# A hybrid diffusion step on one core: the low parts of every second normalised feature tile move from VectorE to GpSimd

## The chip, the cores and the metric

The kernel runs on one core of a Trainium2 chip. Five engines work side by side, each on its own list of instructions: TensorE (PE, matmuls), VectorE (DVE), ScalarE (ACT), GpSimd (POOL) and SyncE (SP), which in this kernel issues nearly all transfers between DRAM and the on-chip memory. An instruction waits until those of other engines that it depends on have ended. The metric is the time of one execution in microseconds, as the device measures it, median of several runs.

## What is computed

One inference step of a two-layer backbone for 640 tokens (128 context tokens, 512 latent ones) of 1024 features. Each layer normalises its input, projects it, runs three token mixers side by side (differential attention, a bidirectional state-space scan, neighbourhood attention), gates and merges them, projects the sum and adds it to the input. The part that the change touches is the first line of each layer; its root mean square is

```python
def _rmsnorm(x, g):
    xf = x.astype(jnp.float32)
    y = xf * lax.rsqrt(jnp.mean(xf * xf, axis=-1, keepdims=True) + EPS)
    return (y * g.astype(jnp.float32)).astype(x.dtype)
```

followed by a scale and a shift per feature that come from a conditioning vector, one pair for context tokens and one for latent tokens. All is in fp32.

## The kernel before

The 640 tokens are columns, the 1024 features are eight tiles of 128 rows ("feature tiles", k = 0 to 7). Columns are worked on in two halves of 320.

TensorE multiplies rounded fp32 numbers (fp32r). To keep fp32 accuracy every operand is held as two: a high part, the value rounded, and a low part, the value less the high part. Each product is three matmuls into the same PSUM bank: high by high, low by high, high by low (`feat`, L162 to L175, and `tok`, L177 to L187). Weights are split on arrival in `weights` (L139 to L151): SyncE fetches `raw` (two buffers), ScalarE rounds it to `hi` (L149), VectorE subtracts to get `lo` (L150). So a third fetch has to wait until the `lo` of two weights earlier is done.

The normalised input is split in `norm_part` (L353 to L366), for each feature tile. VectorE multiplies by scale and by `rb`, which holds the reciprocal root mean square of each column in PSUM (`t`, L362; four buffers). ScalarE adds the shift and rounds (the high part, `hh0` to `hh7`, L364). VectorE adds the shift again and subtracts the high part (the low part, `hl0` to `hl7`, L365). In the first half this is done in two pieces, 128 context columns and 192 latent ones, as their scale and shift differ; in the second in one.

`rms_x` (L322 to L348) makes `rb`: ScalarE squares the feature tiles (`sq`, L330), VectorE sums them (`acc`, L331), TensorE sums over the rows (`ms`, three small matmuls, L337), VectorE scales (`v`, L338), GpSimd raises to the power −1/2 (`r`, L339), VectorE writes it on a diagonal (`d`, L345) and TensorE spreads it over the rows (`rb`, L347).

Two places run this. At the start, layer 0's norm is done for tiles 0 to 3 and then 4 to 7, between the conditioning matmuls (`ada`, L301; `adat`, L307) and the first feature matmuls. At the boundary between the layers, the first half is normalised while the second half's output projection still runs on TensorE; the second half's norm comes behind that projection (`mg` operands in the matmul rows), with only the first half's matmuls of layer 1's first three weights to cover it. There SyncE also stores the residual stream (`xd`) and fetches `vr`, cached values for layer 1's attention, which ScalarE rounds to `vh` (L395). The last norm of the program has its own code and is not touched.

No order is written by hand: the framework's scheduler runs a model of the program and from it lays down one fixed list of instructions per engine. Any change of the program can so change the lists far from it.

Of the kernel before, what the change touches and what calls it, by code (L numbers as in the profile page):

```python
# [11 lines left out]
AF = mybir.ActivationFunctionType  # L12
ALU = mybir.AluOpType
# [110 lines left out]
class Net:  # L124
# [228 lines left out]
    def norm_part(self, l, x, half, ss, rb, ks, p):  # L353
        nc = self.nc
        h = slice(half * 320, half * 320 + 320)
        for k in ks:
            t = p.tile([128, 320], F32, tag="t", name="t", bufs=4)
            hi, lo = (v[:, h] for v in self.h[k])
            for e, s in (((0, slice(0, 128)), (1, slice(128, 320))) if half == 0 else ((1, slice(0, 320)),)):
                n = ss[0].shape[2]  # L360
                shift, scale = (ss[k // n][:, i, k % n, e:e + 1] for i in range(2))
                nc.vector.scalar_tensor_tensor(out=t[:, s], in0=x[k][:, h][:, s], scalar=scale, in1=rb[:, s], op0=ALU.mult,  # L362
                                               op1=ALU.mult)
                nc.scalar.activation(hi[:, s], t[:, s], AF.Identity, bias=shift)  # L364
                nc.vector.scalar_tensor_tensor(out=lo[:, s], in0=t[:, s], scalar=shift, in1=hi[:, s], op0=ALU.add,  # L365
                                               op1=ALU.subtract)  # L366

    def gate_in(self, l, c, p):

# [854 lines left out]
```

## Time and profile before

| | |
|---|---|
| median of 3 runs | 1628.52 us (1628.48 to 1631.17) |
| profiled execution, own time | 1628.46 us |
| its span in the trace | 1626.6 us |
| TensorE busy | 1583.5 us, 97% |
| VectorE busy | 1069.8 us, 66% |
| ScalarE busy | 772.6 us, 47% |
| GpSimd busy | 158.7 us, 10% |
| mean granted clock of TensorE | 0.992 |

The span is the time from the first to the last record of the trace; the execution's own time is 1.9 us longer. Busy shares are means over the whole span, so they say which engine has the least slack, not where. For that the trace is cut into windows, and at the places where TensorE stands idle the timelines of the engines are read: each row gives its start and its length in us, and in brackets how long the engine stood idle before it and which instruction ended that. The granted clock is a share of TensorE's full speed: 1.00 is 2.4 GHz, 0.50 is 1.2 GHz.

### The profile page before, as it was taken

To read this page: it belongs to the slowest core of one execution; us is meant where nothing else is said; L and a number is where in the kernel's file an instruction comes from. 1 tells how busy PE (TensorE), PEld (TensorE's weight loads), DVE (VectorE), ACT (ScalarE), POOL (GpSimd) and SP (SyncE) were. 2 spreads that over 40 slices of the span, in tenths; PEclk is the share of its full clock that TensorE was granted. 3 is DMA by queue.
4 is the path that set the end of the run, shared out by engine and by line. 5 is a ranking of instruction groups with operands and counts; after the bars stand their busy time and mean duration, and the time that the engine had idled before them with its cause. 6 is when DMAs were issued, how large, how long until landed. Compare 5 with 4: busy or idle time off the path is not lost.

```text
span 1626.6 us, 29026 instructions
## 1 busy us (share of the span) xinstructions
PE 1583.5 (97%) x11311; PEld 1507.1 (93%) x11311; DVE 1069.8 (66%) x2290; ACT 772.6 (47%) x1778; POOL 158.7 (10%) x182
## 2 busy tenths in 40 slices
PE   7999999999999999999999999999999999999897
PEld 5999899999999999998989989999999999999896
DVE  5866678667545656756777667766565475576575
ACT  4535654344445454552455475434444455455342
POOL 2003412011000000000000242201010000000000
PEclk9999999999999999999999999999999999999998
DMA  9663235421233433436553222362222443344643
GB/s 336 212 259 101 66 101 168 132 81 52 91 117 103 144 98 123 153 113 236 189 166 122 85 88 83 118 195 71 74 75 83 141 125 90 108 151 138 213 155 124
DMA packets 81672, 214.62 MB, mean 132 GB/s; under 512 B 9728, under 2 KB 25664, under 8 KB 80512
## 3 DMA queue, kind: packets, MB, share of 16 engines
q1 hardware_dynamic: 80624, 211.46, 39.8%
q8 instruction: 89, 1.46, 0.4%
q0 software_dynamic: 480, 0.88, 0.1%
q10 hardware_dynamic: 432, 0.43, 0.1%
q14 instruction: 47, 0.39, 0.1%
HBM read 170.27 MB, written 34.08 MB: 126 GB/s over the span
## 4 chain that ended last, share of the span: by engine, by line
PE 87%; DVE 4%; DMA 3%; issue 2%; ACT 2%; POOL 1%; SPq 0%; POOLq 0%; DVEq 0%; ACTq 0%
PE mm L174 61%; PE mm L186 7%; PE s L958 2%; PE o L982 2%; PE o L540 2%; PE t L974 2%; PE s L525 2%; PE g L787 1%; PE t L532 1%; PE y L800 1%; DMA raw<-in_w_feat 1%; PE y L265 1%; DMA qd<-qr 1%; PE s L521 1%; PE t L741 1%
## 5 line engine op out<-in xcount | busy, mean ns | idle before, releaser
L174 PE MATMUL mm<-hh,hi 128*128 128x320 f32 x1856 | 576.0, 311 | 7.5 <-ACT hh L364 2.8
L174 PE MATMUL mm<-hl,hi 128*128 128x320 f32 x1856 | 578.5, 312 | 0.9 <-DVE hl L365 0.9
L174 PE MATMUL mm<-hh,lo 128*128 128x320 f32 x1856 | 575.2, 310 | 0.7 <-DVE lo L150 0.7
L174 PEld LDWEIGHTS mm<-hh,hi 128*128 128x128 f32 x1856 | 349.4, 188 | 16.8 <-ACT hh L364 3.9
L174 PEld LDWEIGHTS mm<-hl,hi 128*128 128x128 f32 x1856 | 349.5, 188 | 6.8 <-issue 2.7
L174 PEld LDWEIGHTS mm<-hh,lo 128*128 128x128 f32 x1856 | 350.0, 189 | 6.2 <-issue 3.8
L150 DVE TENSOR_TENSOR lo<-raw,hi 128x1024 fp32r<-128x1024 f32 (+2 forms) x194 | 233.4, 1204 | 107.1 <-ACT hi L149 101.4
L149 ACT ACTIVATE hi<-raw 128x1024 fp32r<-128x1024 f32 (+2 forms) x194 | 200.2, 1033 | 189.1 <-PE mm L174 141.0
L174 PE MATMUL mm<-yh,hi 128*128 128x320 f32 x384 | 120.4, 315 | 9.3 <-ACT yh L384 6.2
L174 PE MATMUL mm<-yl,hi 128*128 128x320 f32 x384 | 120.9, 315 | 0.2 <-DVE yl L385 0.2
L174 PE MATMUL mm<-yh,lo 128*128 128x320 f32 x384 | 119.8, 312 | 0.0
L186 PE MATMUL mm<-hi,hh 128*128 128x264 f32 (+1 forms) x320 | 90.6, 284 | 1.8 <-DVE vl L405 1.7
L186 PE MATMUL mm<-lo,hh 128*128 128x264 f32 (+1 forms) x320 | 91.1, 285 | 0.0
L186 PE MATMUL mm<-hi,hl 128*128 128x264 f32 (+1 forms) x320 | 90.4, 283 | 0.0
L534 ACT ACTIVATE ph<-t 128x384 fp32r<-128x384 f32 x64 | 31.4, 490 | 120.0 <-PE t L532 119.9
L174 PEld LDWEIGHTS mm<-yh,hi 128*128 128x128 f32 x384 | 73.1, 191 | 11.3 <-ACT yh L384 6.5
L174 PE MATMUL mm<-mgl,hi 128*128 128x320 f32 x256 | 78.5, 308 | 0.0
L174 PE MATMUL mm<-mgh,lo 128*128 128x320 f32 x256 | 78.0, 307 | 0.0
L174 PE MATMUL mm<-mgh,hi 128*128 128x320 f32 x256 | 77.4, 306 | 0.0
L174 PEld LDWEIGHTS mm<-yl,hi 128*128 128x128 f32 x384 | 73.6, 192 | 0.7 <-DVE yl L385 0.4
L174 PEld LDWEIGHTS mm<-yh,lo 128*128 128x128 f32 x384 | 73.7, 192 | 0.2
L484 DVE TENSOR_REDUCE st<-s 128x2 f32<-128x1536 f32 (+1 forms) x40 | 59.4, 1486 | 21.5 <-PE s L525 19.9
(311 smaller groups left out, 2905.2 us busy)
## 6 DMA issues: line engine op xcount, KB each, us to landing
raw<-in_w_feat SPq DMA_DIRECT2D x110, 512.0 KB, 3.7
aw<-in_w_ada SPq DMA_DIRECT2D x8, 2048.0 KB, 8.1
raw<-in_w_out SPq DMA_DIRECT2D x32, 512.0 KB, 3.6
thd<-th SPq DMA_DIRECT2D x48, 320.0 KB, 2.2
th<-thd SPq DMA_DIRECT2D x48, 320.0 KB, 3.7
raw<-in_w_br SPq DMA_DIRECT2D x24, 512.0 KB, 3.5
accd<-th SPq DMA_DIRECT2D x32, 320.0 KB, 2.9
ac<-accd SPq DMA_DIRECT2D x32, 320.0 KB, 3.8
```

Of the source, the lines that this page charges most:

```text
L149: nc.scalar.activation(hi, raw, AF.Copy)
L150: nc.vector.tensor_tensor(out=lo, in0=raw, in1=hi, op=ALU.subtract)
L174: nc.tensor.matmul(ps, lhsT=s, rhs=r, start=(k == 0 and n == 0), stop=(k == K - 1 and n == 2))
L186: nc.tensor.matmul(ps, lhsT=s, rhs=r, start=(k == 0 and q == 0), stop=(k == 7 and q == 2))
L265: nc.tensor.matmul(ps[32 * g:32 * g + 32, :], lhsT=self.sc[:, 4 * q + i, :], rhs=raw[:, i, 256 * g:256 * g + 256], start=(q + i == 0), sto ...
L484: nc.vector.tensor_reduce(out=st[:, 0:2], in_=s, axis=AX.X, op=ALU.max)
L525: nc.tensor.matmul(s[:, m * 768 + c0:m * 768 + c0 + 512], lhsT=q[:, qs], rhs=ks[m][:, c0:c0 + 512], start=(i == 0), stop=(i == 1))
L534: nc.scalar.activation(ph[dst], pt[:, 0:3, :], AF.Copy)
L540: nc.tensor.matmul(ov[:, 0:256], lhsT=x[:, kt, sv], rhs=q[:, kt, :], start=(kt == 0 and n == 0), stop=(kt == 5 and n == 2))
L958: nc.tensor.matmul(s[:, c0:c0 + n], lhsT=q[:, i * 128:(i + 1) * 128], rhs=ks[j][:, k0:k0 + n], start=(x == 0), stop=(x == 1))
L974: nc.tensor.transpose(pt[:, t, :], e[:, t * 128:(t + 1) * 128], self.ident)
L982: nc.tensor.matmul(out, lhsT=lw, rhs=sel(q), start=(first and x == 0), stop=(last and x == 1))
```

## The change

For odd feature tiles VectorE's subtraction is taken out. ScalarE, after it has written the high part, passes over `t` a second time and writes the shifted value in fp32 in its own place; when the half's columns are done, GpSimd subtracts the high part from it, in one instruction over all 320 columns. Even feature tiles stay as they were. Lines behind the change move down by five.

```diff
--- before.py
+++ after.py
@@ -362,8 +362,13 @@
                 nc.vector.scalar_tensor_tensor(out=t[:, s], in0=x[k][:, h][:, s], scalar=scale, in1=rb[:, s], op0=ALU.mult,
                                                op1=ALU.mult)
                 nc.scalar.activation(hi[:, s], t[:, s], AF.Identity, bias=shift)
-                nc.vector.scalar_tensor_tensor(out=lo[:, s], in0=t[:, s], scalar=shift, in1=hi[:, s], op0=ALU.add,
-                                               op1=ALU.subtract)
+                if k % 2 == 0:
+                    nc.vector.scalar_tensor_tensor(out=lo[:, s], in0=t[:, s], scalar=shift, in1=hi[:, s], op0=ALU.add,
+                                                   op1=ALU.subtract)
+                else:
+                    nc.scalar.activation(t[:, s], t[:, s], AF.Identity, bias=shift)
+            if k % 2:
+                nc.gpsimd.tensor_tensor(out=lo, in0=t, in1=hi, op=ALU.subtract)
 
     def gate_in(self, l, c, p):
```

In all 24 subtractions leave VectorE (two layers, four odd tiles, three pieces), 24 passes come to ScalarE and 16 subtractions to GpSimd. The scheduler lays the lists down anew. They differ in three stretches: from the start to about row 2830 of TensorE's 9965 (start, state-space scan and differential attention of layer 0), at the layer boundary (rows 5049 to 5385), and in some ten rows at the program's end.

SyncE's list at the layer boundary, before: `raw` is a weight, `vr` the cached values, `xd` the residual stream that is stored.

```order
L138 DMA raw_9617<-in_w_feat 128x1024
L138 DMA xd_105<-x4_8876 128x320
L138 DMA raw_9623<-in_w_feat 128x1024
L138 DMA xd_105<-x5_8877 128x320
L138 DMA vr_11152<-in_cvd 128x2x256
L138 DMA raw_9629<-in_w_feat 128x1024
L138 DMA xd_105<-x6_8878 128x320
L138 DMA raw_9920<-in_w_feat 128x1024
```

The same place now; the numbers of the names are shifted by 16, or by 8 for the stores.

```order
L138 DMA raw_9633<-in_w_feat 128x1024
L138 DMA xd_105<-x4_8884 128x320
L138 DMA raw_9639<-in_w_feat 128x1024
L138 DMA xd_105<-x5_8885 128x320
L138 DMA raw_9645<-in_w_feat 128x1024
L138 DMA xd_105<-x6_8886 128x320
L138 DMA vr_11168<-in_cvd 128x2x256
L138 DMA raw_9936<-in_w_feat 128x1024
```

Before, `vr` stood between the second and the third feature weight of layer 1; now the third weight follows the second with only a store between them, and `vr` comes two places later.

TensorE's list at the layer boundary, before: `ms` are the mean squares of the second half, `mm_9701` the bank of the third feature tile.

```order
L174 MATMUL mm_9701<-hh3_87,lo_9632 128x320
L174 MATMUL mm_9701<-hh4_89,hi_9631 128x320
L174 MATMUL mm_9701<-hl4_90,hi_9631 128x320
L174 MATMUL mm_9701<-hh4_89,lo_9632 128x320
L337 MATMUL ms_9540<-masks_133,acc_9517 128x1 x3
L174 MATMUL mm_9701<-hh5_91,hi_9631 128x320
L174 MATMUL mm_9701<-hl5_92,hi_9631 128x320
```

The same instructions now; `mm_9686` is the second feature tile's bank and `mm_9717` the third's.

```order
L174 MATMUL mm_9686<-hh6_93,lo_9642 128x320
L174 MATMUL mm_9686<-hh7_95,hi_9641 128x320
L174 MATMUL mm_9686<-hl7_96,hi_9641 128x320
L174 MATMUL mm_9686<-hh7_95,lo_9642 128x320
L337 MATMUL ms_9552<-masks_133,acc_9529 128x1 x3
L174 MATMUL mm_9717<-hh0_81,hi_9647 128x320
L174 MATMUL mm_9717<-hl0_82,hi_9647 128x320
```

The mean squares stood behind 15 of the third feature tile's 24 matmuls, and now stand ahead of all of them. `rb` stands behind the 24 matmuls in both.

TensorE's list near the program's start, before: `mm_536` is the bank of the third feature tile of layer 0, whose weight is `hi_212`; `adat_450` transposes a conditioning result.

```order
L174 MATMUL mm_522<-hh3_87,hi_206 128x320
L174 MATMUL mm_508<-hl3_88,hi_200 128x320
L174 MATMUL mm_508<-hh3_87,lo_201 128x320
L174 MATMUL mm_522<-hl3_88,hi_206 128x320
L174 MATMUL mm_522<-hh3_87,lo_207 128x320
L174 MATMUL mm_536<-hh0_81,hi_212 128x320
L174 MATMUL mm_536<-hl0_82,hi_212 128x320
L307 MATMUL adat_450<-masks_133,asb_448 128x128
L174 MATMUL mm_536<-hh0_81,lo_213 128x320
```

The same place now, with `mm_540` as that bank.

```order
L174 MATMUL mm_526<-hh3_87,hi_206 128x320
L301 MATMUL ada_320<-aw_442,sc_112 32x128 x8
L174 MATMUL mm_512<-hl3_88,hi_200 128x320
L174 MATMUL mm_512<-hh3_87,lo_201 128x320
L174 MATMUL mm_526<-hl3_88,hi_206 128x320
L174 MATMUL mm_526<-hh3_87,lo_207 128x320
L307 MATMUL adat_454<-masks_133,asb_452 128x128
L301 MATMUL ada_459<-aw_460,sc_112 32x128 x8
L174 MATMUL mm_540<-hh0_81,hi_212 128x320
L174 MATMUL mm_540<-hl0_82,hi_212 128x320
```

The transpose and the first eight conditioning matmuls of the next group (`ada_459`) have come ahead of the third feature tile, and its low-part matmuls give way to those of a tile whose weight is there already (`hi_200`).

## Rows read from the trace of the kernel before

**Rows 1.** The page's part 1: busy us, share, instructions by engine.

```profile
PE 1583.5 (97%) x11311; PEld 1507.1 (93%) x11311; DVE 1069.8 (66%) x2290; ACT 772.6 (47%) x1778; POOL 158.7 (10%) x182
```

**Rows 2.** Windows: length, busy time of each engine (instructions), clock, DMA share, GB/s.

```profile
200.00:300.00 100.00, 98.15 (x665) 93.40 (x665) 76.48 (x156) 44.71 (x107) 17.33 (x17) 1.00 0.44 143
300.00:420.00 120.00, 117.98 (x839) 113.37 (x839) 82.12 (x159) 55.34 (x115) 14.12 (x12) 1.00 0.24 74
744.00:830.00 86.00, 86.00 (x595) 85.74 (x594) 65.94 (x127) 38.77 (x61) 1.53 (x13) 1.00 0.63 207
```

**Rows 3.** The chain of waits from 700 to 1000 us: start, length, what.

```profile
823.60 4.99 DMA raw<-in_w_feat
```

**Rows 4.** Timeline of TensorE around 830 us: start, length, what, idle before.

```profile
829.79 0.42 PE L174 MATMUL mm<-hh,hi 128*128 128x320 f32 x1
...
831.05 0.41 PE L174 MATMUL mm<-hh,lo 128*128 128x320 f32 x1 [0.70 <-DVE lo L150]
...
833.05 0.72 PE L337 MATMUL ms<-masks,acc 128*128 128x1 f32 x6
...
835.64 0.81 PE L347 MATMUL rb<-d,masks 128*128 128x320 f32 x2 [0.42 <-DVE d L345]
837.68 0.71 PE L174 MATMUL mm<-hh,hi 128*128 128x320 f32 x3 [1.24 <-ACT hh L364]
838.92 0.41 PE L174 MATMUL mm<-hl,hi 128*128 128x320 f32 x1 [0.53 <-DVE hl L365]
```

**Rows 5.** Timeline of SyncE's queue around 823 us.

```profile
822.89 0.60 SPq L138 DMA_DIRECT2D vr<-in_cvd  x1
```

**Rows 6.** Timeline of VectorE around 821 to 831 us.

```profile
820.96 1.21 DVE L150 TENSOR_TENSOR lo<-raw,hi 128x1024 fp32r<-128x1024 f32 x1
...
830.91 0.48 DVE L331 TENSOR_TENSOR acc<-acc,sq 128x320 f32<-128x320 f32 x1
```

**Rows 7.** Groups by line and shape, 800 to 850 us: busy, mean ns, idle.

```profile
L150 DVE TENSOR_TENSOR lo<-raw,hi 128x1024 fp32r<-128x1024 f32 x9 | 11.0, 1218 | 5.3 <-ACT hi L149 5.2
...
L364 ACT ACTIVATE hh<-t,ss 128x320 fp32r<-128x320 f32 x8 | 4.0, 556 | 3.0 <-DVE t L362 3.0
...
L365 DVE SCALAR_TENSOR_TENSOR hl<-t,ss,hh 128x192 fp32r<-128x192 f32 x8 | 3.3, 407 | 0.0
...
L365 DVE SCALAR_TENSOR_TENSOR hl<-t,ss,hh 128x128 fp32r<-128x128 f32 x8 | 2.7, 343 | 0.0
```

**Rows 8.** Timeline of GpSimd around 257 and 1044 us.

```profile
257.49 1.83 POOL L439 TENSOR_TENSOR sh<-sh,rope 128x320 f32<-128x320 f32 x1 [1.87 <-DVE sh L438]
...
1044.29 1.15 POOL L439 TENSOR_TENSOR sh<-sh,rope 128x320 f32<-128x320 f32 x1 [3.07 <-DVE sh L438]
```

**Rows 9.** Timeline of VectorE at the same two places.

```profile
257.36 1.23 DVE L150 TENSOR_TENSOR lo<-raw,hi 128x1024 fp32r<-128x1024 f32 x1
...
1044.62 1.90 DVE L150 TENSOR_TENSOR lo<-raw,hi 128x1024 fp32r<-128x1024 f32 x1
```

**Rows 10.** Windows behind three waits of TensorE; PEclk is the granted clock.

```profile
379.40:382.00 2.60, 2.56 (x21) 2.56 (x22) 0.87 (x4) 2.60 (x7) 0.00 (x0) 1.00 0.00 0
839.00:843.00 4.00, 4.00 (x17) 4.00 (x18) 4.00 (x10) 2.36 (x6) 0.00 (x0) 0.57 0.00 0
1070.75:1074.75 4.00, 4.00 (x16) 3.90 (x17) 3.40 (x7) 0.00 (x0) 0.00 (x0) 0.57 0.58 181
```

**Rows 11.** Timeline of TensorE: two waits in the attention stages.

```profile
379.44 0.39 PE L186 MATMUL mm<-hi,hh 128*128 128x256 f32 x1 [1.71 <-DVE vl L405]
...
1070.75 0.41 PE L174 MATMUL mm<-yh,hi 128*128 128x320 f32 x1 [1.81 <-DVE th L1026]
```

**Rows 12.** Timeline of TensorE at the start of the program.

```profile
34.84 0.41 PE L174 MATMUL mm<-hh,hi 128*128 128x320 f32 x1 [2.10 <-ACT hi L149]
...
38.82 1.96 PE L301 MATMUL ada<-aw,sc 128*32 128x128 f32 x64
```

**Rows 13.** Timeline of ScalarE at the start of the program.

```profile
34.16 0.63 ACT L149 ACTIVATE hi<-raw 128x512 fp32r<-128x512 f32 x1 [1.12 <-DMA raw<-in_w_feat]
```

## The prediction

> **What bounds the kernel now.** Read the busy shares first. TensorE is busy 97% of the span; VectorE 66%, ScalarE 47%, GpSimd 10% [rows 1]. The matmuls are not touched, so the change can move only the 43.1 us in which TensorE stands idle (1626.6 − 1583.5) and the time that a lowered clock costs behind a wait. Next look at windows, to see where that idle lies. From 744 to 830 us, where the first half is normalised at the layer boundary, TensorE is busy 86.00 of 86.00 us [rows 2]: nothing that the change saves there shows by itself. In layer 0's state-space scan and attention it stands 1.85 us in the first window and 2.02 in the second [rows 2]. The place to read closely is the second half's normalisation, around 830 to 843 us.
>
> Follow the chain of waits back from there. A feature weight is fetched at 823.60 and its transfer ends 4.99 us later [rows 3]. In TensorE's timeline, two matmuls of the third feature tile run from 829.79 on, then 0.70 us pass waiting for that weight's low part; only after 13 further matmuls come the mean squares at 833.05, then 0.42 us of waiting, `rb` at 835.64, 1.24 us for the first `hh` and 0.53 for the first `hl` [rows 4]. That is 2.89 us of idle in one place. Why was the weight fetched so late? SyncE's queue stood on `vr` until 822.89, for 0.60 us [rows 5], and the weight is right behind it. The weight's own condition, that the low part two weights earlier is done, was met at 820.96 + 1.21 = 822.17 [rows 6]. So it lost 1.43 us to an unrelated load. The last square sum, which needs the copies of that weight out of the way on ScalarE, ends at 830.91 + 0.48 = 831.39 [rows 6], 7.79 us after the fetch.
>
> **What the change costs, part by part.**
>
> 1. *The work itself.* Per odd feature tile and layer, VectorE loses its subtractions: 0.343 + 0.407 us in the first half, about the same as one full-width operation in the second. That is 24 instructions. ScalarE gains 24 second passes, priced by the like first pass (0.556 us for 320 columns) [rows 7], and GpSimd gains 16 subtractions of 320 columns. None of these 16 stands in the trace; the nearest row is GpSimd's `sh` product, two fp32 inputs of the same shape: 1.15 us in one place, 1.83 in another [rows 8]. The 1.83 hold a wait: VectorE had begun a 1024-wide subtraction at 257.36, until 258.59 [rows 9]; if GpSimd works only from there to its own end at 259.32, its work is 0.73. In the other place GpSimd began first, at 1044.29, and the 1024-wide subtraction that VectorE then issued took 1.90 instead of 1.218 [rows 7, 9], 0.68 more. So the price lies between 0.73 and 1.83 us; I take 0.75, as both places point there.
>
> That row is what the Trainium skill, SBUF — State Buffer, "SBUF: two separate sides", calls an exclusive lock: a VectorE operation with two SBUF inputs and a GpSimd operation that reads SBUF shut each other out for the whole instruction. The trace agrees (1.90 for 1.218). It speaks against the change: a subtraction moved to GpSimd would still take VectorE's time wherever the two meet.
>
> By the rows alone: in the first half VectorE gives up 4 x 0.75 = 3.0 us and may be held 4 x 0.75 = 3.0. I therefore count no relief for VectorE, with ends of −3.0 and +4.3 (4 x 1.83 − 3.0). All of it lies below TensorE's 86 full microseconds.
>
> 2. *SyncE's queue.* In the new order the weight stands ahead of `vr`. It is fetched when its buffer is free: 822.17 instead of 823.60 without relief, about 820.7 with half of it. The last square sum then ends at 822.17 + 7.79 = 829.96 (828.5 with relief). `vr` and its high part now come behind on SyncE and ScalarE; `vr` is first used by layer 1's values, far later, so its delay costs nothing.
>
> 3. *TensorE's order.* The mean squares move ahead of the third feature tile, where TensorE arrives at 829.79. They start at about 829.96 and take until 830.4 or so; the tile's 24 matmuls at 0.146 (as from 831.30 to 833.05, 12 of them) are 3.5 us and end by about 833.95. The diagonal for `rb` is ready 835.64 − 833.05 = 2.59 after the mean squares start, at 832.6: hidden under those matmuls. `rb` then ends at 834.75 instead of 835.64 + 0.81 = 836.45. Gain **1.7 us**: the 0.70, the 0.42 and about 0.6 of narrow matmuls and restarts. If the sum is later, TensorE now waits for it with nothing in front: each microsecond past 829.96 costs one until the gain is gone at 1.7.
>
> 4. *After `rb`.* The first four scalings and the first `hl` stay in their order on VectorE, so 1.24 and 0.53 remain. Odd low parts are new here: `hl1` has to pass two ScalarE passes and GpSimd. With `rb` at 834.75 its scaling ends at about 835.8, its second ScalarE pass at 837.3 (fourth in a line of four at 0.46 spacing), GpSimd's subtraction at 838.05 with 0.75 and 839.1 with 1.83. TensorE asks for it after nine matmuls from 837.2: at 838.5 at full clock, 839.6 at half. So 0, up to 0.9 late. `hl3` to `hl7` are asked for later still by 24 matmuls each and are hidden. Behind these subtractions on GpSimd nothing waits at the boundary.
>
> 5. *The clock.* Behind the wait before 839 the granted clock is 0.57 for 4 us, which costs 4 x 0.43 = 1.7 us. It is not so behind every wait: after an idle of 1.71 us at 379.44 it stayed at 1.00; after 1.81 at 1070.75 it fell to 0.57 [rows 10, 11]. What remains here is 1.24 + 0.53 = 1.77 in two pieces, between the two, so whether the clock still falls is open. I leave it falling, and keep a gain of 1.7 as the other end.
>
> 6. *The start.* TensorE waits 2.10 us at 34.84 for ScalarE's copy of a weight [rows 12]. The copy starts at 34.16, behind 1.12 us of waiting for the transfer [rows 13], so nothing upstream of it gets faster. The new order puts one quarter of a group of 64 conditioning matmuls (1.96 us at 38.82 [rows 12], so 0.5) ahead of that wait: −0.5. ScalarE's added passes may delay the copy by one pass, +0.2 to +0.5. I take −0.3, between −0.8 and +0.6.
>
> 7. *Layer 0's scan and attention.* From the start to about a quarter of TensorE's list the scheduler wrote another order, though no work changes. I price it at 0, between −1.5 and +2.0: of the 3.87 us of idle there now [rows 2] less than half may be won, and about as much again be added. From layer 1's scan on the order is the same.
>
> Sum: −1.7 − 0.3 + 0 = −2.0. Against the profiled execution's own 1628.46 (0.06 below the median 1628.52) that is **1626.5 us**.
>
> **Rivals.** What a measurement of this kernel tells from no change is about 0.2%, 3.3 us: faster is below 1625.3, slower above 1631.8.
>
> *The clock stays up too* (0.25). Idle shorter than the 1.77, or split otherwise, as at 379.44: another 1.7 us, 1624.8. For it: the 0.70 and 0.42 waits ahead are gone. Against it: 1.77 is nearer to the 1.81 that fell.
>
> *The gain is eaten* (0.17). The new early order or a square sum that ends near 831.4 gives back the 1.7 to 2: 1628.5. For it: without relief on VectorE the sum comes at 829.96, already 0.17 after TensorE gets there. Against it: `vr` is plainly what the weight waited for.
>
> *The lock at its dear end* (0.08). Each subtraction holds VectorE 1.83: the weight is fetched at 822.17 + 4.3 = 826.5, the sum ends at 834.3, `rb` ends 3.4 later at 837.7, 1.2 after before; with `hl1` 0.9 late and the start's −0.3 that is 1628.46 + 1.8 = 1630.3. The row with 1.90 for 1.218 speaks for 0.7 rather than 1.8. The Trainium skill's SBUF — State Buffer, "SBUF: two separate sides", leads here only if GpSimd keeps the shared way for the whole 1.83.
>
> *Slower* (0.10). Layer 0's new attention order runs into waits of layer 1's kind, for a gate value that comes back from DRAM: 1.81 idle and the fallen clock after it, 1.81 + 1.7 = 3.5 us each [rows 10, 11]. One of them leaves 1626.5 + 3.5 = 1630.0; it decides from two, 1626.5 + 7.0 = 1633.5. For it: layer 1 has the same code in another order and pays it. Against: the two stages of layer 0 show no fall now.
>
> **How the numbers follow.** Forecast 0.40 (1624.9 to 1627.8 by its own terms), clock 0.25, eaten 0.17, lock 0.08, slower 0.10. Faster: the clock case with most of its spread and the edge of the forecast, 0.30. Slower: the slower case and the tail of the lock, 0.11. Same: the rest, 0.59. The range for 8 in 10 leaves out the slower case and the far end of the clock case: 1622.8 to 1630.8.
>
> **What would show it.** Right: the weight's fetch no longer behind `vr`, at 822.2 or before relative to the same matmul; no wait of the third feature tile for a low part; `rb` following matmuls without a gap; 1.24 and 0.53 still there. GpSimd subtractions of 0.73 to 0.8 when alone; VectorE operations lengthened beside them. Wrong: a wait of the mean squares for the square sum, matmuls that wait for an odd `hl` by GpSimd, or a fall of the clock in layer 0 between 200 and 420 us.

## The result, and the profile after

The changed kernel takes 1641.79 us (median of 6 runs, 1638.36 to 1643.32) against 1628.39 for the kernel before: ratio 1.0078, interval 1.0063 to 1.0092. It is slower by some 13 us, and the forecast of 1626.5 was wrong. The profiled execution takes 1642.57 with a span of 1640.8.

Landmarks that both traces have tell where the time went. The first is the first score matmul of layer 0's neighbourhood attention, before and after, 15.6 us later:

```profile
507.50 0.49 PE L958 MATMUL s<-ks,qh 128*128 128x256 f32 x2
```

```profile
523.11 0.48 PE L963 MATMUL s<-ks,qh 128*128 128x256 f32 x2
```

The boundary's first `rb`, before and after, is 16.3 later:

```profile
804.76 0.70 PE L347 MATMUL rb<-d,masks 128*128 128x320 f32 x2
```

```profile
821.07 0.70 PE L347 MATMUL rb<-d,masks 128*128 128x320 f32 x2
```

The second `rb` starts at 835.64 [rows 4] and now at 850.26, 14.6 later. So all of the loss but 0.7 us is there before 507 us, in layer 0, and between its two `rb` the boundary gains 1.7.

Not all of that gain stays. The first `w` of layer 1's scan (L766, now L771) starts at 896.43 and at 911.64, 15.2 later: up to there the boundary is worth 1.1 us. TensorE has no new wait on that stretch; what gives the 0.6 back is not shown. The end of the span is 14.2 later, and most of that last microsecond is the clock: it fell behind the wait of 1.81 at 1070.75 [rows 10, 11], and behind the same wait of the changed kernel, 2.04 at 1086.19, it stayed at 1.00.

The windows of the changed kernel that answer to the first two of [rows 2] (length, busy time of PE, PEld, DVE, ACT, POOL, then the granted clock):

```profile
200.00:300.00 100.00, 90.11 (x576) 84.24 (x576) 74.63 (x160) 43.31 (x109) 18.19 (x18) 0.93 0.35 113
300.00:420.00 120.00, 118.03 (x831) 113.12 (x831) 79.38 (x153) 50.47 (x104) 14.46 (x11) 1.00 0.28 86
```

From 200 to 300 us TensorE stands idle for 9.89 us instead of 1.85, and the clock is 0.93 instead of 1.00, which costs another 7 us of work. Those 15 us are nearly all of the loss. The clock is low in two places, 0.72 from 245 to 257 us and 0.76 from 290 to 304, 3.4 us each. The timeline of TensorE there, all waits above 0.2 us:

```profile
247.85 0.66 PE L832 MATMUL t<-masks,ysb 128*128 128x128 f32 x4 [3.58 <-DVE ysb L829]
...
250.56 0.80 PE L505 MATMUL s<-kx,qx 64*128 64x128 f32 x4 [2.05 <-ACT qx L440]
252.06 0.61 PE L174 MATMUL mm<-hh,hi 128*128 128x320 f32 x1 [0.71 <-DVE sh L443]
...
295.13 0.63 PE L174 MATMUL mm<-yh,hi 128*128 128x320 f32 x1 [3.39 <-DVE th L1031]
```

The first two waits belong to the end of the state-space scan: its last output `y` goes through VectorE, ScalarE and GpSimd (`ysb`, normalised), is transposed (`t`, L832) and split again (`yh` on ScalarE). The kernel before ran the same chain without a wait at the transposes. VectorE's and ScalarE's instructions of this chain are neither added nor changed by the edit. What changed is what TensorE has to do meanwhile. Counted in the two lists: before, 64 matmuls of other work stand between the last `y` and the transposes, and 27 between the transposes and the first scores; after, 20 and 0.

The chain from the last `y` to the scaled `ysb`, before: TensorE's last `y` group and VectorE's last step.

```profile
228.65 1.89 PE L800 MATMUL y<-xt,ma 128*128 128x64 f32 x16
```

```profile
236.38 0.48 DVE L824 TENSOR_SCALAR ysb<-ysb,rs 128x512 f32<-128x512 f32 x1 [0.72 <-POOL rs L195]
```

And after:

```profile
240.29 1.00 PE L805 MATMUL y<-xt,ma 128*128 128x64 f32 x8
```

```profile
247.31 0.48 DVE L829 TENSOR_SCALAR ysb<-ysb,rs 128x512 f32<-128x512 f32 x1 [0.72 <-POOL rs L195]
```

From the end of `y` to the end of the scaling it is 236.86 − 230.54 = 6.3 us before and 247.79 − 241.29 = 6.5 after: the chain is as long as it was. At 0.146 us each, 43 matmuls cover 6.3 us. Before there were 64; now 20, which is 23 too few, 3.4 us. The wait is 3.58.

The second wait has another form. The scores do not use `y`; they wait for `kx` and `qx`, two copies that stand behind `yh` in ScalarE's list. After:

```profile
249.27 0.91 ACT L839 ACTIVATE yh<-yf 128x128 fp32r<-128x128 f32 x4 [2.86 <-DVE yf L834]
250.08 0.25 ACT L440 ACTIVATE kx<-mm 128x128 f32<-128x128 f32 x1
250.24 0.26 ACT L440 ACTIVATE qx<-mm 128x128 f32<-128x128 f32 x1
```

From the end of the transposes to the scores this chain takes 2.05 us, and no matmul covers it. Before, `qx` waited for the last of the 27 matmuls itself, so those 27 are not the cover that the chain needs:

```profile
244.31 0.28 ACT L435 ACTIVATE qx<-mm 128x128 f32<-128x128 f32 x1 [1.62 <-PE mm L174]
```

At the layer boundary the forecast's account holds. Timeline of TensorE after, answering to [rows 4]:

```profile
846.09 0.72 PE L337 MATMUL ms<-masks,acc 128*128 128x1 f32 x6
...
850.26 0.70 PE L347 MATMUL rb<-d,masks 128*128 128x320 f32 x2
852.20 0.70 PE L174 MATMUL mm<-hh,hi 128*128 128x320 f32 x3 [1.23 <-ACT hh L364]
853.44 0.60 PE L174 MATMUL mm<-hl,hi 128*128 128x320 f32 x1 [0.54 <-DVE hl L366]
```

The waits of 0.70 and 0.42 are gone, `rb` follows the matmuls without a gap, and 1.23 and 0.54 remain. SyncE's queue there shows why [rows 5]; the third feature weight is fetched at 837.79, 16.7 us after the first `rb` instead of 18.8. Of these 2.1 us, 1.4 are `vr`; the rest is the low part that frees the weight's buffer, which ends 16.7 us after that `rb` instead of 17.4:

```profile
837.79 0.33 SPq L138 DMA_DIRECT2D raw<-in_w_feat  x1
838.25 0.34 SPq L138 DMA_DIRECT2D xd<-x  x1
839.20 0.60 SPq L138 DMA_DIRECT2D vr<-in_cvd  x1
```

### The profile page after: what moved, and what is told of

Read it like the earlier page. It is cut to its first block, busy times and chain, and to the rows that moved or that the text cites. A ratio compares the mean times of both kernels' runs of the same rounds, so it can differ in the third digit from the quotient of the medians.

```text
span 1640.8 us, 29047 instructions
## 1 busy us (share of the span) xinstructions
PE 1592.6 (97%) x11311; PEld 1511.1 (92%) x11311; DVE 1062.7 (65%) x2266; ACT 780.9 (48%) x1802; POOL 175.9 (11%) x198
## 4 chain that ended last, share of the span: by engine, by line
PE 84%; DVE 6%; DMA 3%; issue 3%; ACT 3%; POOL 1%; SPq 0%; POOLq 0%; DVEq 0%; ACTq 0%
PE mm L174 58%; PE mm L186 7%; PE s L963 2%; PE o L987 2%; PE t L979 2%; PE o L545 2%; PE s L530 1%; DMA qd<-qr 1%; PE g L792 1%; PE y L805 1%; PE t L537 1%; PE y L265 1%; POOL sh L444 1%; PE s L526 1%; ACT hi L149 1%
```

## The experiments

Nine kernels were run, each beside the kernel before on the same chip. Runs 1 to 4, 5 to 7, and 8 and 9 each have a measurement of it (1628.35, 1628.00, 1628.06), to which the ratios refer. Two theories: *order*, that layer 0's rewritten lists cost the time, whatever is done at the start; and *work*, that ScalarE's and GpSimd's new instructions at the start do, by holding VectorE or by coming late.

| run | median us | ratio (interval) | matmuls before transposes / scores |
|---|---|---|---|
| kernel before | 1628.4 | 1 | 64 / 27 |
| changed kernel | 1641.79 | 1.0078 (1.0063 to 1.0092) | 20 / 0 |
| 1 boundary only | 1626.09 | 0.9987 (0.9975 to 0.9998) | 64 / 27 |
| 2 start only | 1644.68 | 1.0099 (1.0082 to 1.0116) | 20 / 0 |
| 3 even tiles at the start | 1626.24 | 0.9988 (0.9978 to 0.9997) | 64 / 27 |
| 4 tiles 1 and 3 at the start | 1637.99 | 1.0068 (1.0053 to 1.0084) | 45 / 0 |
| 5 order of writing only | 1641.06 | 1.0081 (1.0064 to 1.0097) | 46 / 0 |
| 6 ScalarE's pass, no GpSimd | 1632.61 | 1.0031 (1.0020 to 1.0042) | 45 / 0 |
| 7 `vr` on GpSimd's queue | 1626.94 | 0.9996 (0.9987 to 1.0005) | 64 / 27 |
| 8 whole change, other list | 1627.83 | 1.0001 (0.9992 to 1.0009) | 69 / 11 |
| 9 boundary, GpSimd twice | 1629.49 | 1.0013 (1.0002 to 1.0023) | 64 / 27 |

**Runs 1 and 2: which place.**

```diff
 # run 1
-                if k % 2 == 0:
+                if l == 0 or k % 2 == 0:
...
-            if k % 2:
+            if l and k % 2:
 # run 2
-                if k % 2 == 0:
+                if l or k % 2 == 0:
...
-            if k % 2:
+            if l == 0 and k % 2:
```

> Only the norm of layer 1 (at the layer boundary) is split between ScalarE and GpSimd; the norm at the start is done as before. TensorE's list of layer 0 is then row for row that of the kernel before. Theory 'order': the loss of 13.4 us sits in layer 0's rewritten list, so here it is gone and what the boundary gives stays: rb 1.7 us earlier, less or more some 0.6 for the clock, so about 1626 (ratio 0.998 to 0.999). Theory 'GpSimd's work': the boundary's eight subtractions cost their part (half the sixteen), about 1635.

> Only the norm of layer 0 (at the start) is split between ScalarE and GpSimd; the boundary is as before. TensorE's list of layer 0 is row for row that of the changed kernel. Both theories that put the loss before 420 us say +15 us, about 1644. If the boundary carried the loss: about 1626 to 1629.

Measured 1626.09 and 1644.68. The boundary alone is a gain of 2 us that is just clear of no change; the start alone loses 16. The 2.9 us between run 2 and the changed kernel have the size of the boundary's gain, but are not shown to be that: in the profiles run 2 is already 2.7 us behind at the boundary's first `rb` (823.76 and 821.07).

**Run 3: the same work at the start, another list.**

```diff
-                if k % 2 == 0:
+                if k % 2 == 1 - l:
...
-            if k % 2:
+            if k % 2 == l:
```

> As the changed kernel, but at the start the even feature tiles are the ones whose low parts GpSimd makes, so ScalarE, GpSimd and VectorE have the same number of instructions of the same shapes. The scheduler's list of layer 0 then differs from that of the kernel before in 80 rows of TensorE, all but the first hundreds the same; 64 matmuls stand between the scan's last output and the transposes that wait for it, as before, against 20 in the changed kernel. 'Order': about 1626 to 1628, no wait of TensorE between 240 and 252 us. 'Work' (GpSimd's subtractions at the start, or VectorE held by them): the loss stays, 1640 or more, or more still as the first hl is now GpSimd's.

Measured 1626.24, with the same eight subtractions on GpSimd at the start. In 230 to 260 us TensorE has the waits of the kernel before and no others:

```profile
244.16 0.49 PE L505 MATMUL s<-kx,qx 64*128 64x128 f32 x4 [0.37 <-ACT qx L440]
244.88 0.38 PE L174 MATMUL mm<-hh,hi 128*128 128x320 f32 x1 [0.22 <-DVE sh L443]
```

'Work' falls with this run: as many instructions of the same shapes are there, and cost nothing that shows. The gate value is waited for here too, 1.56 us at 279.77; the clock stays at 1.00 behind it.

**Run 4: fewer tiles, part of the cover back.**

```diff
-                if k % 2 == 0:
+                if l == 0 and k > 3 or k % 2 == 0:
...
-            if k % 2:
+            if k % 2 and not (l == 0 and k > 3):
```

> As the changed kernel, but at the start only tiles 1 and 3 are split off to GpSimd (four of the eight subtractions), 5 and 7 are done as before. The list of layer 0 is nearly that of the changed kernel, but 45 matmuls cover the scan's last output instead of 20. 'Order': the wait of 3.58 us for the scan's output is gone (45 matmuls at 0.146 are 6.6 us, the output takes 6.3 to 6.8), the waits of 2.05 + 0.71 and 3.39 behind it stay with their clock falls: 10 us over the boundary-only kernel, about 1636. 'Work': half the work at the start, half the loss, and in all three waits alike: about 1634.

Measured 1637.99, 2 us above the figure for 'order' and 4 above that for 'work'. The waits tell the two apart: the 3.58 is gone, as the count of matmuls gave, and the others stay where 'work' would have halved them all:

```profile
246.89 0.49 PE L505 MATMUL s<-kx,qx 64*128 64x128 f32 x4 [2.05 <-ACT qx L440]
248.40 0.38 PE L174 MATMUL mm<-hh,hi 128*128 128x320 f32 x1 [1.02 <-DVE sh L443]
...
290.36 0.63 PE L174 MATMUL mm<-yh,hi 128*128 128x320 f32 x1 [2.71 <-DVE th L1031]
```

**Run 5: no change of work at all.** An edit of the kernel before:

```diff
-                        self.norm_part(0, x, half, nxt, rb[half], range(4, 8), np_)
+                        self.norm_part(0, x, half, nxt, rb[half], (7, 6, 5, 4), np_)
```

> The kernel before with one loop of the start written in another order: feature tiles 7, 6, 5, 4 instead of 4, 5, 6, 7. No instruction is added, removed or moved to another engine. The scheduler's list of layer 0 comes out as in the run with tiles 1 and 3 at the start: 46 matmuls under the scan's last output, none between the transposes and the first attention scores (27 before). 'Order': waits of about 2 + 1 us around 247 and of 2.7 to 3.4 at 290 with their clock falls, about 8 to 10 us over the kernel before, 1636 to 1638. 'Work': the work is that of the kernel before, so 1628.

Measured 1641.06: as slow as the changed kernel, with every instruction of the kernel before on its own engine. It is 3 us more than expected. The expectation was taken from run 4, which has the boundary's gain and this one not; that is a part of it. In the profiles run 5 is also 3.1 us behind run 4 ahead of the boundary (first `rb` at 818.23 and 815.13), with a clock of 0.95 and 0.99 in the first two windows of [rows 2], where run 4 has 0.97 and 1.00.

```profile
246.53 0.49 PE L500 MATMUL s<-kx,qx 64*128 64x128 f32 x4 [2.05 <-ACT qx L435]
248.04 0.38 PE L174 MATMUL mm<-hh,hi 128*128 128x320 f32 x1 [1.02 <-DVE sh L438]
...
290.52 0.64 PE L174 MATMUL mm<-yh,hi 128*128 128x320 f32 x1 [2.92 <-DVE th L1026]
```

**Run 6: ScalarE's pass without GpSimd.** An edit of the changed kernel:

```diff
-                nc.gpsimd.tensor_tensor(out=lo, in0=t, in1=hi, op=ALU.subtract)
+                nc.vector.tensor_tensor(out=lo, in0=t, in1=hi, op=ALU.subtract)
```

> The changed kernel with VectorE, not GpSimd, subtracting the high part over all 320 columns; ScalarE's second pass stays. GpSimd has the work of the kernel before. The list of layer 0 has 45 matmuls under the scan's last output and none before the scores. 'Order': 1634 to 1638, with the two waits of the run with tiles 1 and 3 at the start. 'GpSimd's work': 1628 or less.

Measured 1632.61: slower than before without any new work on GpSimd, but outside both ranges. The waits before the scores are the same 2.05 and 1.02; the third one, for the gate value, is 0.56 here instead of 2.7. The expectation had taken that one over from run 4, though the count of matmuls at the scan does not govern it.

**Run 8: the whole change with another list.** An edit of the changed kernel, at both halves:

```diff
-                    self.norm_part(0, x, 0, nxt, rb[0], range(4), np_)
+                    self.norm_part(0, x, 0, nxt, rb[0], (0, 2, 1, 3), np_)
...
-                    self.norm_part(0, x, 1, nxt, rb[1], range(4), np_)
+                    self.norm_part(0, x, 1, nxt, rb[1], (0, 2, 1, 3), np_)
```

> The whole change (odd tiles at both places on ScalarE and GpSimd), with one loop of the start written in another order: tiles 0, 2, 1, 3 instead of 0, 1, 2, 3. The same instructions on the same engines as in the changed kernel; the list of layer 0 comes out otherwise, with 69 matmuls under the scan's last output (20 in the changed kernel, 64 before) and 11 before the attention scores (0, 27 before). 'Order': no wait at the transposes, 27 - 11 = 16 matmuls too few before the scores, so a wait of 1 to 1.5 us there; in all 1627 to 1632, at least 10 us under the changed kernel's 1641.8. 'Work': 1640 or more, as the changed kernel.

Measured 1627.83, 14 us under the changed kernel with the same instructions on the same engines. The transposes wait no more. The wait before the scores is 0.44, and 1.02 stand behind them; their sum lies in the 1 to 1.5 us that were expected, but not for the reason given. 11 matmuls are 1.6 us of the chain's 2.05, which leaves 0.44; 16 too few would have been 2.3.

```profile
245.30 0.49 PE L505 MATMUL s<-kx,qx 64*128 64x128 f32 x4 [0.44 <-ACT qx L440]
246.81 0.39 PE L174 MATMUL mm<-hh,hi 128*128 128x320 f32 x1 [1.02 <-DVE sh L443]
```

**Run 7: what gives the boundary its gain.** An edit of the kernel before: only `vr`'s first load of layer 1 leaves SyncE's queue.

```diff
-        self.dma(vr, a["cvd"][l, :, :, hp * 256:(hp + 1) * 256])
+        (nc.gpsimd if l and hp == 0 else nc.sync).dma_start(out=vr, in_=a["cvd"][l, :, :, hp * 256:(hp + 1) * 256])
```

> The kernel before with one edit: the first load of vr in layer 1 is issued by GpSimd instead of SyncE; nothing is split differently. The third feature weight is then no longer behind vr in SyncE's queue, and the mean squares stand after 12 of the third tile's matmuls. Theory 'queue' for the boundary: no wait for that weight's low part (0.70 us before), rb 1.1 to 1.7 us earlier, 1626.5 to 1627.5. Theory 'relief of VectorE' (the boundary's gain comes from the subtractions that left VectorE): no gain here, 1628.4. Layer 0's list is that of the kernel before.

The median is 1626.94, but its interval holds no change, so the time alone decides nothing. The trace does. The boundary's first `rb` starts at 805.48 in this run, 0.72 after that of the kernel before (804.76), and the second at 834.71 instead of 835.64: 0.93 + 0.72 = 1.65 us gained in between. TensorE's timeline has no wait for the weight's low part, as with the change, though no subtraction has moved:

```profile
832.09 0.72 PE L337 MATMUL ms<-masks,acc 128*128 128x1 f32 x6
834.71 0.81 PE L347 MATMUL rb<-d,masks 128*128 128x320 f32 x2
836.75 0.72 PE L174 MATMUL mm<-hh,hi 128*128 128x320 f32 x3 [1.23 <-ACT hh L364]
```

So the queue, not relief of VectorE, frees the boundary. How much that is depends on the execution it is compared with: the two `rb` lie 29.2 us apart here and in the changed kernel, and 30.9 in the kernel before, but 30.3 and 30.2 in runs 2 and 5, whose boundary is that of the kernel before and where the wait for the low part is 0.22 and 0.14 instead of 0.70. The gain between the two is thus 1.0 to 1.7 us.

**Run 9: is GpSimd's work free?** An edit of run 1's kernel:

```diff
                 nc.gpsimd.tensor_tensor(out=lo, in0=t, in1=hi, op=ALU.subtract)
+                nc.gpsimd.tensor_tensor(out=lo, in0=t, in1=hi, op=ALU.subtract)
```

> The boundary-only kernel with each of GpSimd's eight subtractions issued twice in a row (the second writes the same values), so 8 more at 0.87 us alone. 'Hidden': the first half's four lie under the projection's matmuls; in the second half the first odd low part comes 0.9 us later and delays TensorE by 0 to 0.9 us, the others by nothing: 1626 to 1627.5. 'Lock': VectorE is held by every one of them beside its own operations, 3.5 us in each half; the weight's fetch moves back by up to 3.5, the square sum with it, and rb's gain of 1.7 us is gone: 1628 to 1630.

Measured 1629.49, 3.4 above run 1: the side of the lock. In the profiles the two `rb` are 30.5 us apart, against 29.2 in run 1. VectorE's first four low parts (two of 128 columns, two of 192; a row shows the first shape) take 3.90 us beside GpSimd's subtractions, where the changed kernel's take 1.89 and eight of them took 2.45 before. Before, and in this run:

```profile
809.43 2.45 DVE L365 SCALAR_TENSOR_TENSOR hl<-t,ss,hh 128x128 fp32r<-128x128 f32 x8
```

```profile
809.92 3.90 DVE L366 SCALAR_TENSOR_TENSOR hl<-t,ss,hh 128x128 fp32r<-128x128 f32 x4
```

TensorE then waits for low parts of weights while the first half is normalised, which were hidden before, and for GpSimd in the second half:

```profile
817.04 0.41 PE L174 MATMUL mm<-mgh,lo 128*128 128x320 f32 x1 [0.18 <-DVE lo L150]
821.29 0.41 PE L174 MATMUL mm<-mgh,lo 128*128 128x320 f32 x1 [0.47 <-DVE lo L150]
...
841.04 0.42 PE L174 MATMUL mm<-hl,hi 128*128 128x320 f32 x1 [0.57 <-POOL hl L372]
```

Runs 1 and 3 beat both kernels, by 2 us against the one before, just clear of no change, and by 15 against the changed one.

## Why the prediction was wrong

The step that failed is the seventh, "Layer 0's scan and attention". It was priced "at 0, between −1.5 and +2.0", by the idle that the old order leaves. That is no bound: an order that waits little says nothing of what its successor uncovers. The measured price is about +15 us: 15.6 at 507 us, of which the start has 0.4; 8.0 of idle and 7 of clock. The cause is the new list, as runs 3, 5 and 8 show: it leaves too little work under two chains that TensorE waits for. The rival *Slower* had the stage, the fallen clock and the sign, but put the waits at the gate value alone, asked for two of them and got 0.10. Of the three places that wait, one is that gate value (3.39 us); the scan's output is the larger part (3.58 + 2.05 + 0.71).

The first wait could have been sized before the run. The old trace shows a chain of 6.3 us from the last `y`; the two lists show 64 matmuls on top of it before and 20 after; 23 too few at 0.146 make 3.4 us. That the others and the clock could have been sized too is not shown. I had seen that the lists differ over their first 2830 rows and did not count at the places where TensorE waits for another engine's chain.

The other steps, one by one:

- *SyncE's queue and TensorE's order* (steps 2 and 3): right in the mechanism. Gain of `rb` 1.7 forecast; 16.3 − 14.6 = 1.7 measured, and 1.65 by the queue alone (run 7). Against runs 2 and 5 it is 1.0, and 0.6 of it is gone by 911 us, a loss that the sum had no term for.
- *After `rb`* (4): right. 1.23 and 0.54 stay, no TensorE wait for an odd `hl` at the boundary.
- *The work* (1): GpSimd's subtraction alone takes 0.88 us, where 0.75 was taken and 0.73 to 0.8 was to be the sign. The lock on VectorE is there. Its relief was taken as nil; the low part that frees the third weight's buffer ended 0.7 us earlier, by relief or by VectorE's new order, and run 7 gains as much without it. That it is hidden holds for one subtraction per tile, not for two (run 9).
- *The clock* (5): left falling, and it fell: 0.81 and 0.76 in the two windows of 4 us from 851, 0.19 x 4 + 0.24 x 4 = 1.7 us in all. That was one of two outcomes: in the profiles of runs 3, 4 and 8, with the same edit at the boundary, it stayed at 1.00. In layer 0 it was missed with the waits.
- *The start* (6): −0.3 forecast; matched by their names, TensorE's matmuls between 40 and 120 us come 0.4 us later instead, inside the bounds, but by luck: the terms were others. The wait of 2.10 fell to 0.5, and in the first 40 us TensorE stands idle 2.7 us less, while the clock is 0.87 instead of 0.96, which costs 3.6.

The gate value's wait has a likely cause in SyncE's list that no run tried by itself. Each trace has a place where TensorE waits longest for a gate value, 1.04 us before and 3.39 after (not the same feature tile). The chain of waits there, before and after, is a store and a load that follows it:

```profile
273.23 2.75 DMA accd<-th
276.00 3.76 DMA th<-thd
```

```profile
285.50 5.64 DMA accd<-th
291.16 3.31 DMA th<-thd
```

Now a weight's fetch at 286.71 stands between the two, and the store takes twice as long; before, the weight came behind the load, at 278.52. The other traces go with this: runs 2, 4 and 5 have the fetch between the two, stores of 5.0 to 5.7 us and waits of 2.7 to 3.2; in all others it stands behind the load and the wait is 1.56 at most, also in run 6, whose matmuls before the scores are as few as theirs. Against it, a store of run 7 takes 5.87 us with no fetch between it and its load. So the cause is argued from the traces, not shown.

## What to carry to other kernels

Where a scheduler lays down the lists, an edit at one place is an edit of everything up to the next point where the lists meet again; compare them there before pricing the edit. At each place where the busiest engine waits for a chain of others, take the chain's length from the old trace and count, in the new list, the independent work that stands over it: too few instructions times their duration is the new wait. Here that gave the first wait to 0.2 us, and the second only where the chain itself, and not the old cover, was the measure (run 8); what the clock takes behind a wait comes on top. And to learn whether an edit or its order costs the time, permute the order of writing of something harmless (run 5) or of the edit itself (run 8).

## What the runs showed of the hardware

GpSimd's subtractions and VectorE's operations on two on-chip (SBUF) inputs hold each other up. GpSimd alone takes 0.88 us for 320 columns. Beside VectorE it reads as 1.90, and VectorE's operations stretch at the same time; changed kernel, at the boundary's first half:

```profile
824.66 1.90 POOL L371 TENSOR_TENSOR hl<-t,hh 128x320 fp32r<-128x320 f32 x1 [7.01 <-ACT t L369]
...
827.60 0.88 POOL L371 TENSOR_TENSOR hl<-t,hh 128x320 fp32r<-128x320 f32 x1 [1.04 <-ACT t L369]
```

```profile
824.61 1.22 DVE L150 TENSOR_TENSOR lo<-raw,hi 128x1024 fp32r<-128x1024 f32 x1
825.74 1.89 DVE L366 SCALAR_TENSOR_TENSOR hl<-t,ss,hh 128x128 fp32r<-128x128 f32 x4
```

VectorE's subtraction holds GpSimd until 825.83; GpSimd then works until 826.56, 0.73 us, and VectorE's four low parts take 1.89 instead of some 1.2 (half of the 2.45 before). The 0.73 and the 0.88 differ by 0.15; that a part of GpSimd's time passes while it waits is a reading of these two numbers, not shown otherwise. Not every operation is held: the GpSimd row at 827.60 runs beside VectorE's `x` (L1061) and `t` (L362), which read one input from PSUM, and these take 0.54 and 0.33 us, their usual length. The Trainium skill, SBUF — State Buffer, "Who interferes with whom", says that a VectorE instruction with two SBUF inputs contends with a GpSimd instruction that reads SBUF; the rows agree, 1.90 for 0.88.

The clock's fall behind a wait near 1.8 us is not settled by the wait's length. With 1.23 to 1.24 and 0.53 to 0.55 at the same place it fell in run 1 and not in run 7, in this order (windows of 4 us after the waits); it fell in the changed kernel too, and not in runs 3, 4 and 8:

```profile
838.00:842.00 4.00, 3.86 (x16) 3.86 (x17) 3.49 (x8) 3.97 (x10) 2.71 (x3) 0.57 0.00 0
```

```profile
838.00:842.00 4.00, 4.00 (x27) 4.00 (x28) 4.00 (x10) 2.36 (x6) 0.00 (x0) 1.00 0.00 0
```

That is 4 x 0.43 = 1.7 us from one profiled execution to another, as much as the boundary gains between its two `rb`.
